# Seven-product blocks: products that need no sum first, K before Q in a level, four state updates to a bank

## The chip, the cores and the metric

The kernel runs on one core of a Trainium2 chip, as one launch. The metric is the device time of that launch in microseconds. Engines are called as in the profile: PE is TensorE (PEld its weight loads), DVE is VectorE, ACT is ScalarE, POOL is GpSimd, and SP is SyncE, which here issues most of the loads. GpSimd's queue issues the stores.

## What is computed

A backbone of two layers over 1024 latent tokens and 256 context tokens of width 1024. Layer one (neighbourhood attention beside a bidirectional mLSTM) is not touched by the change. Layer two is a bidirectional HGRN2 mixer with 16 heads of 128 keys and 128 values. Cut to what matters:

```python
def _c_mixer(h_lat, h_ctx, w_in, lb, h_norm, w_out, need_ctx):
    q, f_fwd, f_bwd, i, z = _split_cols(h @ w_in, C_SIZES)       # five blocks of 2048 columns
    f = lb + (1.0 - lb) * jax.nn.sigmoid(f_pre)                  # per direction; k = 1 - f
    ...
    # per head, per direction, chunkwise over tokens:
    S = exp(bL) * S + k_decayed.T @ v                            # the state update
    o = (q * exp(b)) @ S + a @ v
    ...
    return (rms(o) * silu(z)) @ w_out
```

All arithmetic is float32. A product of float32 matrices is made from three matmuls of split operands: each operand is kept as a high part (hh, wh: the value rounded to the matmul's format) and a low part (hl, wl: the rest), and the sum hi*hi + hi*lo + lo*hi is accumulated in PSUM. In the profile these three are the lines L131 to L133 of the helper `dense`.

## The kernel before, in words

**What sets the order.** The program is traced by a tile framework. Every instruction has a priority, by its place in the program; blocks under `urgent` come ahead of everything else. At build time a planner runs the instructions through a simulated timeline and, on each engine, always takes the ready instruction of the highest priority. On the chip each engine then works through its list strictly in order, with semaphores between engines. Buffers are rings: `self.t(pool, shape, dtype, tag, bufs)` takes the next free one of `bufs` slots of that tag, and whoever reuses a slot waits for the last reader. `self.ps(tag, shape)` takes one PSUM bank (128 x 512 float32). There are two banks for "mm", two for "tr", and in each phase some for other tags: four for "x" in the seven-product stage, three for "s" and one for "acc" in the heads. When a pool is opened over the memory of pools that were closed, its first users wait; `reuse_waits="tile"` (new in the change) makes that wait go by tile, not by pool.

**End of layer one.** The last loop of layer one (lines 1671 to 1683) forms, for each of ten token tiles in the order 8, 9, 4, 5, 6, 7, 0, 1, 2, 3, the output product, the norm and the transposed, split input of layer two: `hh` and `hl`, eight blocks of 128 rows by 1280 tokens. Pools "op0" and "wo1" hold its tiles; "st" and "sx" of the next stage are laid over them. `hg_f(0)` (line 970) then makes the backward gate of head 0 into the tile F; its half F[:, 0] is loaded only later, by `hg_proj` (line 986).

**The seven-product stage** (`hg_wide`, line 1043) computes q and the forward f for all heads: 16 units, two heads of one kind each, over a 2 x 2 blocking of weights by 512 rows and 128 columns and of h by 512 rows and 512 tokens. A unit uses seven products of blocks in place of eight. Three of them take a raw block of h, with the weight pieces (0,0), (1,0) and t4; the others take one of S1 to S4, which are sums of blocks of h, made once by `half_sums` (line 998), with the pieces t1, t2, t3 and (1,1). t1 to t4 are sums of weight blocks, made on POOL from the raw ones (line 1072). S1, S2 and S4 are chained on DVE, S3 on POOL; each is then split into a high part (ACT, line 73) and a low part (DVE, line 74), and so is each weight piece. Raw weights, t-sums and the scratch of the half sums share one ring "br" of 10 slots. `more` (line 1086) loads and splits weight pieces three products ahead. A product is 12 matmuls of 512 columns; an f unit also has four context parts of 12 matmuls of 256 columns (`cpart`). A bank such as pb takes product after product, with a DVE add that reads it between them.

**The heads.** After that come 16 heads, one after another: `hg_intra` with seven levels (`hg_level`, line 1275), `hg_vz` (v and z by matmuls), `hg_close` (transposes of K), `hg_ctx`, `hg_scan`. In a level, ACT copies the needed half of K to gksel (line 1286), PE forms 16 strips (line 1256) into one "s" bank, DVE multiplies the needed halves of Q and K by the totals (line 1303), and then folds the totals (line 1307). The matmuls of `hg_vz` and `hg_f` of the next head lie between the strips as the planner fits them in.

**The scan** (`hg_scan`, line 1316) goes over eight chunks of 128 tokens. Backward, for c = 7 to 1: a matmul u (line 1323) into an "s" bank of its own, then a DVE operation that makes the next state from the last one and u (line 1325). Forward, for c = 0 to 7: three matmuls of the output (lines 1334 to 1336) into a quarter of the "acc" bank, the forward u (line 1339) into an "s" bank, and its update (line 1341). After each four chunks ACT sums the squares (line 1350) and DVE multiplies by z (line 1354), which frees the z tile: gz has one buffer, and the next head's z waits for it (line 1189).

In layer one, `ml_yt` (lines 696 to 705) is of use to the prediction: for j in 0, 1 it transposes into half j of one "tr" bank (line 701) and reads that half by ACT (line 702).

Of the kernel before, what the change touches and what calls it, by code (L numbers as in the profile page):

```python
# [10 lines left out]
F32 = mybir.dt.float32  # L11
# [34 lines left out]
class Prog:  # L46
# [948 lines left out]
        return dict(F=F, Fc=Fc, q=q)  # L995


    def half_sums(self, pool, tp):
        nc = self.nc
        hh, hl = self.hh, self.hl  # L1000
        S = {n: [self.t(pool, [P, 4, 512], F32R, f"st{n}{c}", 1) for c in "hl"] for n in range(1, 5)}

        def A(t, c, j):
            s = slice(512 * t, 512 * t + 512)
            return hh[:, 4 * c + j, s].bitcast(F32), hl[:, 4 * c + j, s].bitcast(F32)

        def done(n, j, x):
            self.split(S[n][0][:, j, :], S[n][1][:, j, :], x)

        def pair(eng, out, x, y, op):  # L1010
            e = self.t(tp, [P, 512], F32, "br", self.brs)
            eng.tensor_tensor(out=out, in0=x[0], in1=y[0], op=op)
            eng.tensor_tensor(out=e, in0=x[1], in1=y[1], op=op)
            eng.tensor_tensor(out=out, in0=out, in1=e, op=ALU.add)

        tt = nc.vector.tensor_tensor
        s1 = []
        for j in range(4):
            s1.append(self.t(tp, [P, 512], F32, "br", self.brs))
            pair(nc.vector, s1[j], A(1, 0, j), A(1, 1, j), ALU.add)  # L1020
            done(1, j, s1[j])
        s3 = []
        for j in range(2):
            s3.append(self.t(tp, [P, 512], F32, "br", self.brs))
            pair(nc.gpsimd, s3[j], A(0, 0, j), A(1, 0, j), ALU.subtract)
        for j in range(4):
            for x in A(0, 0, j):
                tt(out=s1[j], in0=s1[j], in1=x, op=ALU.subtract)
            done(2, j, s1[j])
        for j in range(4):  # L1030
            if j > 1:
                s3.append(self.t(tp, [P, 512], F32, "br", self.brs))
                pair(nc.gpsimd, s3[j], A(0, 0, j), A(1, 0, j), ALU.subtract)
            done(3, j, s3[j])
        for j in range(4):
            h, l = A(0, 1, j)
            tt(out=s1[j], in0=h, in1=s1[j], op=ALU.subtract)
            tt(out=s1[j], in0=s1[j], in1=l, op=ALU.add)
            done(4, j, s1[j])
        return S  # L1040


    def hg_wide(self, sp, tp):
        nc, a = self.nc, self.a
        hh, hl = self.hh, self.hl
        self.brs = 10
        S = self.half_sums(sp, tp)
        add = lambda out, x, y: nc.vector.tensor_tensor(out=out, in0=x, in1=y, op=ALU.add)

        def X(n):  # L1050
# [9 lines left out]
        def raws(kind, i):  # L1060
            c0 = (2048 if kind == "f" else 0) + 2 * i * P
            b = {}
            for r, c in ((0, 0), (0, 1), (1, 1), (1, 0)):
                b[(r, c)] = self.t(tp, [P, 512], F32, "br", self.brs)
                nc.sync.dma_start(
                    out=b[(r, c)].rearrange("p (k f) -> p k f", f=P),
                    in_=a["wc"][r * 512 : r * 512 + 512, c0 + c * P : c0 + c * P + P].rearrange("(k p) f -> p k f", p=P),
                )

            def sub(x, y, out=None):  # L1070
                o = self.t(tp, [P, 512], F32, "br", self.brs) if out is None else out
                nc.gpsimd.tensor_tensor(out=o, in0=x, in1=y, op=ALU.subtract)
                return o

            b["t1"] = sub(b[(0, 1)], b[(0, 0)])
            b["t2"] = sub(b[(1, 1)], b["t1"])
            b["t3"] = sub(b[(1, 1)], b[(0, 1)], None if kind == "f" else b[(0, 1)])
            b["t4"] = sub(b[(1, 0)], b["t2"])
# [14 lines left out]
            del queue[:n]  # L1093

        more(3)
        for u, (kind, i) in enumerate(units):
            def form(n):
                more(1)
                return forms.pop((u, n))
# [15 lines left out]
            def tail(t, c, ps, x):  # L1115
                o = self.t(tp, [P, 512], F32, "ct", 2)
                add(o, ps, x)
                finish(t, c, o)

            ctx = {}  # L1120

# [39 lines left out]
            prod(pc, w, 4, False)  # L1161
            tail(0, 1, pc, u2)
            cpart(1, w, 4, True)


# [109 lines left out]
    def hg_level(self, H, lev, pool):  # L1275
# [4 lines left out]

        pick = lambda t: _skew(t[:, 0, :].rearrange("p (b s i) -> p b s i", s=2, i=h), 2, n)
        out = self.ps("s", [P, 8, 64])
        with self.urgent():
            if lev < 6:
                ksel = self.t(pool, [P, n], F32, "gksel", 1)
                m = nc.scalar.copy(ksel.rearrange("p (b s i) -> p b s i", s=2, i=h), pick(K))  # L1286
                if lev == 5:
                    self.level = m
            for c in range(8):
                for b in range(2):  # L1290
                    o = c * P + b * 64
                    r = out[:, c, :]
                    if lev < 6:
                        r = r.rearrange("p (b s i) -> p b s i", s=2, i=h)
                        lhsT, rhs = ksel[:, o : o + 64], pick(Q)[:, o // (2 * h) : (o + 64) // (2 * h)]
                    else:
                        lhsT = K[:, b, o : o + 64]
                        rhs = Q[:, 1 - b, c * P + (1 - b) * 64 : c * P + (2 - b) * 64]
                    self.strip(r, b, lhsT, rhs)
            for t, o, step in ((Q, n + 1, -n - 1), (K, 1, n - 1)):  # L1300
                v = bass.AP(t.tensor, t.offset, [list(t.ap[0]), [n + h, 2], [2 * h, nb], [1, h]])
                tot = bass.AP(Tt.tensor, Tt.offset + o, [list(Tt.ap[0]), [step, 2], [2, nb], [0, h]])
                nc.vector.tensor_tensor(out=v, in0=v, in1=tot, op=ALU.mult)  # L1303
# [3 lines left out]
            nc.vector.tensor_tensor(out=H["T"][:, :, 0:nb], in0=Tv[:, :, :, 0], in1=Tv[:, :, :, 1], op=ALU.mult)  # L1307
# [8 lines left out]
    def hg_scan(self, st, H, S, pool):  # L1316
# [2 lines left out]
        Sf, Sb = S  # L1319
        sb = {7: Sb}  # L1320
        for c in range(7, 0, -1):
            u = self.ps("s", [P, P])
            nc.tensor.matmul(u, lhsT=H["kn"][c // 4][1][:, c % 4, :], rhs=v[:, c, :], start=True, stop=True)
            s = self.t(pool, [P, P], F32, "gS1", 10)
            nc.vector.scalar_tensor_tensor(
# [3 lines left out]
        for c in range(8):  # L1329
            cs = slice(c * P, (c + 1) * P)  # L1330
            if c % 4 == 0:
                o4 = self.ps("acc", [P, 4, P])
            o = o4[:, c % 4, :]
            nc.tensor.matmul(o, lhsT=H["A"][:, c, :], rhs=v[:, c, :], start=True, stop=False)  # L1334
            nc.tensor.matmul(o, lhsT=H["Q"][:, 0, cs], rhs=sb[c], start=False, stop=False)  # L1335
            nc.tensor.matmul(o, lhsT=H["Q"][:, 1, cs], rhs=Sf, start=False, stop=True)
            if c < 7:
                u = self.ps("s", [P, P])
                nc.tensor.matmul(u, lhsT=H["kn"][c // 4][0][:, c % 4, :], rhs=v[:, c, :], start=True, stop=True)
                s = self.t(pool, [P, P], F32, "gS0", 2)  # L1340
                nc.vector.scalar_tensor_tensor(
# [66 lines left out]
    def build(self):  # L1408
        tc, nc, a = self.tc, self.nc, self.a
        dma = nc.sync.dma_start  # L1410
        with ExitStack() as es:
# [271 lines left out]

            with l1:
                FF = self.hg_f(0, None, wf)
                with tc.tile_pool(name="st", bufs=1) as sp, tc.tile_pool(name="sx", bufs=1) as tp, self.pp.phase(x=4):
                    self.hg_wide(sp, tp)
                    col = lambda i: a["wc"][:, i * 2048 : i * 2048 + P]
                    wv = self.wblock(
                        self.wp, "w", [col(3), col(4)], KD, 256, [tp, self.brs, "br"], ring=self.slabs  # L1690
                    )
                pool = l1.enter_context(tc.tile_pool(name="hg", bufs=2))
                self.rawp = pool
                banks = l1.enter_context(ExitStack())
                banks.enter_context(self.pp.phase(s=3, acc=1))
# [343 lines left out]
```

## Time and profile before

| | us |
|---|---|
| median of three runs | 3423.19 |
| lowest and highest | 3419.49, 3425.61 |
| the profiled execution | 3423.08 |
| its span, first to last instruction | 3421.3 |
| seven-product stage, steady part | from about 1846 to 2199 |
| heads | from about 2199 |

In the profile's views a time is in us from the span's start. A timeline row is: start, length, engine, line, operation, out<-in, shapes, count, and in brackets the idle time of the engine before it with what ended it. In a waits row stand who waited, for whom, the total, how many times, and the longest. Names are those of the program's tiles: "br" the ring of raw weights, "st1h" the high part of S1, "gK", "gQ", "gS" the K, Q and state of a head, "x", "mm", "s", "acc", "tr" the PSUM tags.

### The profile page before, as it was taken

The page shows a single profiled execution, that of the slowest core. Times are in us where ns is not written, and L with a number is a line of the kernel's source. Part 1 is how long each engine was busy: PE and PEld are TensorE (multiplying, and loading weights), DVE is VectorE, ACT ScalarE, POOL GpSimd, SP SyncE. Part 2 cuts the span into 40 slices and gives each one's busy share as a digit, 9 for nine tenths or more (in the row PEclk, how much of TensorE's full clock was granted, in tenths as well). Part 3 has the DMA queues.
Part 4 walks back from the last instruction along what each step waited for, and adds up shares of the span by engine and source line. Part 5 has one row for each costly group of instructions (what it writes and reads, how often), then busy time and mean ns, then how long its engine had stood idle before and what let it go on. Part 6 is the DMA issues. An engine that isn't in the chain of part 4 may idle for free. (4 is left out here: it accounts for less than half of the span.)

```text
span 3421.3 us, 64930 instructions
## 1 busy us (share of the span) xinstructions
PE 3324.6 (97%) x24814; PEld 2927.6 (86%) x24814; DVE 2186.1 (64%) x4965; ACT 1454.6 (43%) x3389; POOL 834.7 (24%) x1215
## 2 busy tenths in 40 slices
PE   7999999999999999999997999999999999999999
PEld 6699899988899888898885888888888889889887
DVE  5346666666645576686667555665676576667757
ACT  5335554445534444454453333333333333333343
POOL 2222222222221121221015333112332242233110
PEclk9999999999999999999998999999999999999999
DMA  7612322223234443444742322322222233333357
GB/s 246 233 50 82 86 83 72 82 71 91 82 93 128 127 136 107 124 142 140 244 123 74 105 101 98 106 67 83 88 94 91 81 98 84 85 86 92 83 173 207
DMA packets 338103, 379.82 MB, mean 111 GB/s; under 512 B 34600, under 2 KB 269800, under 8 KB 336768
## 3 DMA queue, kind: packets, MB, share of 16 engines
q1 hardware_dynamic: 286032, 236.73, 23.6%
q0 software_dynamic: 51760, 138.94, 12.8%
q8 instruction: 195, 3.19, 0.4%
q14 instruction: 116, 0.95, 0.1%
HBM read 272.31 MB, written 103.08 MB: 110 GB/s over the span
## 5 line engine op out<-in xcount | busy, mean ns | idle before, releaser
L131 PE MATMUL mm<-wh,hh 128*128 128x256 f32 (+1 forms) x1504 | 464.2, 309 | 1.9 <-DVE graw L1535 0.7
L132 PE MATMUL mm<-wl,hh 128*128 128x256 f32 (+1 forms) x1504 | 462.9, 308 | 0.0
L133 PE MATMUL mm<-wh,hl 128*128 128x256 f32 (+1 forms) x1504 | 459.9, 306 | 0.0
L131 PE MATMUL mm<-hh,wh 128*128 128x512 f32 (+1 forms) x1096 | 400.3, 365 | 12.8 <-ACT wh L73 12.2
L133 PE MATMUL mm<-hh,wl 128*128 128x512 f32 (+1 forms) x1096 | 396.1, 362 | 3.1 <-DVE wl L74 3.1
L132 PE MATMUL mm<-hl,wh 128*128 128x512 f32 (+1 forms) x1096 | 396.9, 362 | 1.6 <-DVE hl L318 1.6
L131 PEld LDWEIGHTS mm<-wh,hh 128*128 128x128 f32 x1504 | 283.6, 189 | 21.1 <-ACT ev L352 3.4
L132 PEld LDWEIGHTS mm<-wl,hh 128*128 128x128 f32 x1504 | 283.6, 189 | 12.6 <-issue 0.7
L133 PEld LDWEIGHTS mm<-wh,hl 128*128 128x128 f32 x1504 | 283.5, 188 | 12.0 <-issue 0.5
L131 PE MATMUL mm<-wzh,hh 128*128 128x256 f32 x960 | 275.0, 287 | 0.7 <-DVE gz L1189 0.4
L132 PE MATMUL mm<-wzl,hh 128*128 128x256 f32 x960 | 275.2, 287 | 0.0
L133 PE MATMUL mm<-wzh,hl 128*128 128x256 f32 x960 | 274.8, 286 | 0.0
L131 PEld LDWEIGHTS mm<-hh,wh 128*128 128x128 f32 x1096 | 207.5, 189 | 47.9 <-ACT wh L73 12.6
L133 PEld LDWEIGHTS mm<-hh,wl 128*128 128x128 f32 x1096 | 207.2, 189 | 33.8 <-DVE wl L74 3.8
L132 PEld LDWEIGHTS mm<-hl,wh 128*128 128x128 f32 x1096 | 207.5, 189 | 31.9 <-DVE hl L318 4.3
L1286 ACT COPY gksel<-gK 128x1024 f32<-128x1024 f32 x96 | 110.8, 1154 | 193.8 <-PE s L1256 112.9
L131 PEld LDWEIGHTS mm<-wzh,hh 128*128 128x128 f32 x960 | 183.4, 191 | 2.7 <-DVE gz L1189 0.9
L132 PEld LDWEIGHTS mm<-wzl,hh 128*128 128x128 f32 x960 | 183.6, 191 | 1.6
L133 PEld LDWEIGHTS mm<-wzh,hl 128*128 128x128 f32 x960 | 183.4, 191 | 0.9
L1303 DVE TENSOR_TENSOR gQ<-gQ,gF 128x1024 f32<-128x1024 f32 x112 | 142.0, 1268 | 46.5 <-PE s L1256 46.1
L74 DVE TENSOR_TENSOR wl<-wraw,wh 128x512 fp32r<-128x512 f32 x176 | 120.0, 689 | 77.9 <-ACT wh L73 75.4
L1303 DVE TENSOR_TENSOR gK<-gK,gF 128x1024 f32<-128x1024 f32 x112 | 143.0, 1276 | 5.3 <-DVE gF L1307 0.5
(557 smaller groups left out, 8607.9 us busy)
## 6 DMA issues: line engine op xcount, KB each, us to landing
wraw<-in_wab_dram SPq DMA_DIRECT2D x108, 256.0 KB
wraw<-yd SPq DMA_DIRECT2D x92, 256.0 KB
br<-in_wc_dram SPq DMA_DIRECT2D x64, 256.0 KB
md<-ev POOLq DMA_DIRECT2D x60, 256.0 KB, 2.7
wraw<-in_wc_dram SPq DMA_DIRECT2D x120, 128.0 KB
mloz<-md SPq DMA_DIRECT2D x40, 256.0 KB
s<-gyt POOLq DMA_DIRECT2D x36, 256.0 KB, 5.0
adar<-in_wada_dram SPq DMA_DIRECT2D x16, 512.0 KB
```

The lines of the kernel that those rows point to most:

```text
L74: nc.vector.tensor_tensor(out=lo, in0=x, in1=hi.bitcast(F32), op=ALU.subtract)
L131: mm(ps, lhsT=lh(k), rhs=rh(k), start=(start and k == 0), stop=False, skip_group_check=skip)
L132: mm(ps, lhsT=lh(k), rhs=rl(k), start=False, stop=False, skip_group_check=skip)
L133: m = mm(ps, lhsT=ll(k), rhs=rh(k), start=False, stop=(stop and k == nk - 1), skip_group_check=skip)
L1286: m = nc.scalar.copy(ksel.rearrange("p (b s i) -> p b s i", s=2, i=h), pick(K))
L1303: nc.vector.tensor_tensor(out=v, in0=v, in1=tot, op=ALU.mult)
```

## The change

Four groups of edits:

- **Start of a unit.** The products go (0,0), (1,0), t4, then t2, t3, t1, then (0,1) for f and (1,1); before it was (0,0), t2, (1,0), t3, t1, t4. t4 gets a bank of its own (pd, tag "mm") instead of adding to pb. The raw blocks are loaded in the order (0,0), (1,0), (0,1), (1,1); f units come before q units.
- **Half sums.** The first three weight pieces are asked for before `half_sums` is called. The half sums no longer use the ring "br" (now 11 slots): the running sums sit in the two free halves of F[:, 0] and in u2 and u3, those of S3 in "co". The S tiles are laid out in the order 4, 3, 1, 2. Pools "st", "sx" and "hg" get `reuse_waits="tile"`. The number of operations is as before.
- **A level.** For levels 0 to 5 the multiplication of K is traced straight after the copy to gksel; Q's stays behind the strips. At level 6 the order is Q, then K.
- **The scan.** The u of chunks 7 to 4 share one "s" bank and those of 3 to 1 another; forward, 0 to 3 one and 4 to 6 another. The matmuls and the DVE updates themselves are as before.

The diff, cut to its core:

```diff
     def half_sums(self, pool, tp, F):
-        S = {n: [self.t(pool, [P, 4, 512], F32R, f"st{n}{c}", 1) for c in "hl"] for n in range(1, 5)}
+        S = {n: [self.t(pool, [P, 4, 512], F32R, f"st{n}{c}", 1) for c in "hl"] for n in (4, 3, 1, 2)}
+        x = [F[:, 0, 0:512], F[:, 0, 512:1024]] + [self.t(tp, [P, 512], F32, n, 1) for n in ("u2", "u3")]
+        def chain(eng, out, x0, x1, *rest):
+            eng.tensor_tensor(out=out, in0=x0, in1=x1[0], op=x1[1])
+            for y, op in rest:
+                eng.tensor_tensor(out=out, in0=out, in1=y, op=op)
+        for j in range(4):
+            (h, l), (h2, l2) = A(1, 0, j), A(1, 1, j)
+            chain(nc.vector, x[j], h, (l, add), (h2, add), (l2, add))
+            done(1, j, x[j])
+        for j in range(4):
+            h, l = A(0, 0, j)
+            chain(nc.vector, x[j], x[j], (h, sub), (l, sub))
+            done(2, j, x[j])
+        for j in range(4):
+            (h, l), (h2, l2) = A(0, 0, j), A(1, 0, j)
+            y = self.t(tp, [P, 512], F32, "co", 2)
+            chain(nc.gpsimd, y, h, (l, add), (h2, sub), (l2, sub))
+            done(3, j, y)
         for j in range(4):
             h, l = A(0, 1, j)
+            chain(nc.vector, x[j], h, (x[j], sub), (l, add))
+            done(4, j, x[j])
...
     def hg_wide(self, sp, tp, F):
-        self.brs = 10
-        S = self.half_sums(sp, tp)
+        self.brs = 11
...
-        units = [(kind, i) for i in range(8) for kind in "qf"]
-        order = lambda kind: [(0, 0), "t2", (1, 0), "t3", "t1", "t4"] + ([(0, 1)] if kind == "f" else []) + [(1, 1)]
+        units = [(kind, i) for i in range(8) for kind in "fq"]
+        order = lambda kind: [(0, 0), (1, 0), "t4", "t2", "t3", "t1"] + ([(0, 1)] if kind == "f" else []) + [(1, 1)]
...
         more(3)
+        S = self.half_sums(sp, tp, F)
...
-            p1, u2, u3 = [self.t(tp, [P, 512], F32, n, 1) for n in ("p1", "u2", "u3")]
-            pa, pb, pc = self.ps("mm", [P, 512]), self.ps("x", [P, 512]), self.ps("x", [P, 512])
+            p1, u2, u3 = [self.t(tp, [P, 512], F32, n, 2 if n == "p1" else 1) for n in ("p1", "u2", "u3")]
+            pa, pd = [self.ps("mm", [P, 512]) for _ in range(2)]
+            pb, pc = [self.ps("x", [P, 512]) for _ in range(2)]
             w = form((0, 0))
             prod(pa, w, (0, 0), True)
             nc.scalar.copy(p1, pa)
             cpart(0, w, 0, False)
-            prod(pb, form("t2"), 2, True)
-            add(u2, pb, p1)
             w = form((1, 0))
             prod(pa, w, (0, 1), False)
             finish(0, 0, pa)
             cpart(0, w, 4, True)
+            prod(pd, form("t4"), (1, 1), True)
+            prod(pb, form("t2"), 2, True)
+            add(u2, pb, p1)
             prod(pb, form("t3"), 3, False)
             add(u3, pb, p1)
+            tail(1, 0, pd, u3, p1)
             prod(pc, form("t1"), 1, True)
-            tail(1, 1, pc, u3)
-            prod(pb, form("t4"), (1, 1), False)
-            tail(1, 0, pb, p1)
+            tail(1, 1, pc, u3, u3)
...
     def hg_level(self, H, lev, pool):
+        def update(t, o, step):
...
+                update(K, 1, n - 1)
             for c in range(8):
                 for b in range(2):
...
-            for t, o, step in ((Q, n + 1, -n - 1), (K, 1, n - 1)):
...
+            update(Q, n + 1, -n - 1)
+            if lev == 6:
+                update(K, 1, n - 1)
...
     def hg_scan(self, st, H, S, pool):
         for c in range(7, 0, -1):
-            u = self.ps("s", [P, P])
+            if c in (7, 3):
+                u4 = self.ps("s", [P, 4, P])
+            u = u4[:, c % 4, :]
...
             if c % 4 == 0:
                 o4 = self.ps("acc", [P, 4, P])
+                u4 = self.ps("s", [P, 4, P])
...
-                u = self.ps("s", [P, P])
+                u = u4[:, c % 4, :]
...
-                with tc.tile_pool(name="st", bufs=1) as sp, tc.tile_pool(name="sx", bufs=1) as tp, self.pp.phase(x=4):
-                    self.hg_wide(sp, tp)
+                with tc.tile_pool(name="st", bufs=1, reuse_waits="tile") as sp, tc.tile_pool(name="sx", bufs=1, reuse_waits="tile") as tp, self.pp.phase(x=4):
+                    self.hg_wide(sp, tp, FF[0])
...
-                pool = l1.enter_context(tc.tile_pool(name="hg", bufs=2))
+                pool = l1.enter_context(tc.tile_pool(name="hg", bufs=2, reuse_waits="tile"))
```

More of the change, by code (lines that the diff above doesn't have):

```diff
@@ L995, in hg_proj, with half_sums @@
         return dict(F=F, Fc=Fc, q=q)
-    def half_sums(self, pool, tp):
+    def half_sums(self, pool, tp, F):
         nc = self.nc
         hh, hl = self.hh, self.hl
-        S = {n: [self.t(pool, [P, 4, 512], F32R, f"st{n}{c}", 1) for c in "hl"] for n in range(1, 5)}
+        S = {n: [self.t(pool, [P, 4, 512], F32R, f"st{n}{c}", 1) for c in "hl"] for n in (4, 3, 1, 2)}
+        x = [F[:, 0, 0:512], F[:, 0, 512:1024]] + [self.t(tp, [P, 512], F32, n, 1) for n in ("u2", "u3")]
         def A(t, c, j):
@@ L1004, in A @@
             s = slice(512 * t, 512 * t + 512)
[L1005 to L1014, printed above, removed]
@@ L1016, in half_sums @@
-        tt = nc.vector.tensor_tensor
-        s1 = []
-        for j in range(4):
[L1019 to L1025, printed above, removed]
+            return [y[:, 4 * c + j, s].bitcast(F32) for y in (hh, hl)]
@@ new lines, in chain, with done @@
+        def chain(eng, out, x0, x1, *rest):
+            eng.tensor_tensor(out=out, in0=x0, in1=x1[0], op=x1[1])
+            for y, op in rest:
+                eng.tensor_tensor(out=out, in0=out, in1=y, op=op)
+        def done(n, j, y):
+            self.split(S[n][0][:, j, :], S[n][1][:, j, :], y)
+        add, sub = ALU.add, ALU.subtract
+        for j in range(4):
+            (h, l), (h2, l2) = A(1, 0, j), A(1, 1, j)
+            chain(nc.vector, x[j], h, (l, add), (h2, add), (l2, add))
+            done(1, j, x[j])
@@ L1026, in half_sums @@
         for j in range(4):
-            for x in A(0, 0, j):
-                tt(out=s1[j], in0=s1[j], in1=x, op=ALU.subtract)
-            done(2, j, s1[j])
+            h, l = A(0, 0, j)
+            chain(nc.vector, x[j], x[j], (h, sub), (l, sub))
+            done(2, j, x[j])
         for j in range(4):
[L1031 to L1034, printed above, removed]
+            (h, l), (h2, l2) = A(0, 0, j), A(1, 0, j)
@@ L1035, in half_sums, with hg_wide @@
+            y = self.t(tp, [P, 512], F32, "co", 2)
+            chain(nc.gpsimd, y, h, (l, add), (h2, sub), (l2, sub))
+            done(3, j, y)
         for j in range(4):
             h, l = A(0, 1, j)
-            tt(out=s1[j], in0=h, in1=s1[j], op=ALU.subtract)
-            tt(out=s1[j], in0=s1[j], in1=l, op=ALU.add)
-            done(4, j, s1[j])
+            chain(nc.vector, x[j], h, (x[j], sub), (l, add))
+            done(4, j, x[j])
         return S
-    def hg_wide(self, sp, tp):
+    def hg_wide(self, sp, tp, F):
@@ L1062, in raws @@
             b = {}
-            for r, c in ((0, 0), (0, 1), (1, 1), (1, 0)):
+            for r, c in ((0, 0), (1, 0), (0, 1), (1, 1)):
                 b[(r, c)] = self.t(tp, [P, 512], F32, "br", self.brs)
@@ L1113, in finish, with tail @@
                 nc.gpsimd.dma_start(out=d[h, :, 512 * t : 512 * t + 512], in_=o)
[L1115 to L1118, printed above, removed]
+            def tail(t, c, ps, x, out):
+                add(out, ps, x)
+                finish(t, c, out)
             ctx = {}
@@ L1161, in hg_wide @@
             prod(pc, w, 4, False)
-            tail(0, 1, pc, u2)
+            tail(0, 1, pc, u2, u2)
             cpart(1, w, 4, True)
@@ L1282, in hg_level @@
         out = self.ps("s", [P, 8, 64])
+        def update(t, o, step):
+            v = bass.AP(t.tensor, t.offset, [list(t.ap[0]), [n + h, 2], [2 * h, nb], [1, h]])
+            tot = bass.AP(Tt.tensor, Tt.offset + o, [list(Tt.ap[0]), [step, 2], [2, nb], [0, h]])
+            nc.vector.tensor_tensor(out=v, in0=v, in1=tot, op=ALU.mult)
         with self.urgent():
```

5 lines of the change are left out of this document (1 added, 4 removed).

## The prediction, made before the change was run

> **What bounds the kernel now.** I read the page first, then a table of four windows around layer two, then the waits of TensorE and of the DMA queue there, then timelines of one head.
>
> ```profile
> span 3421.3 us, 64930 instructions
> ## 1 busy us (share of the span) xinstructions
> PE 3324.6 (97%) x24814; PEld 2927.6 (86%) x24814; DVE 2186.1 (64%) x4965; ACT 1454.6 (43%) x3389; POOL 834.7 (24%) x1215
> ```
>
> TensorE is the bound: 97% busy. The change adds and removes no matmul, so it can only move idle time of TensorE, and time at a reduced clock. The windows (columns: length, busy time and count of each engine, granted clock, DMA share, GB/s) show where these lie in layer two:
>
> ```profile
> 1798.00:1812.30 14.30, 10.29 (x36) 6.20 (x34) 12.02 (x20) 6.74 (x20) 10.93 (x11) 0.88 0.05 19
> 1812.30:1846.00 33.70, 12.96 (x30) 8.69 (x29) 29.98 (x38) 12.73 (x24) 21.09 (x11) 0.60 0.22 63
> 1846.00:2199.00 353.00, 353.00 (x1730) 297.07 (x1729) 199.77 (x280) 124.18 (x214) 127.54 (x139) 1.00 0.30 100
> 2199.00:3217.00 1018.00, 981.77 (x9931) 903.28 (x9929) 685.86 (x1087) 365.12 (x775) 278.80 (x384) 1.00 0.30 87
> ```
>
> Row three is the steady part of the seven-product blocks, without idle time. About 384 of its 1730 matmuls are the half-wide context ones; counted half, a 512-wide matmul takes 353/1538 = 0.23 us. Row two is the blocks' start: 30 matmuls, 6.9 us of work, in 33.7 us, so 26.8 us are lost. Row four is the heads: 36 us idle.
>
> **Part one: the blocks' start.** What TensorE waits for there (who, whom, us in total, times, longest), and the DMA queue's longest wait for a POOL instruction:
>
> ```profile
> PE mm L131 <- ACT wh L73: 12.2, 1, 12.2
> PE x L131 <- ACT wh L73: 5.4, 2, 3.9
> PE mm L133 <- DVE wl L74: 3.1, 1, 3.1
> ```
>
> ```profile
> SPq L1065 <- POOL br L1014: 18.6, 1, 18.6
> ```
>
> The first weight's DMA waits until a POOL sum (L1014) gives up a "br" slot, since the half sums use that ring and come first in program order. The weight, its split and the first matmul follow late: 12.2 us. Then the clock is 0.60 and the weight pieces come one by one.
>
> The change issues the first block's four DMAs before the sums, gives the sums other scratch (u2, u3 and the free half of F), and starts the block with (0,0), (1,0) and t4, which read h alone. When may those DMAs start? The same pool's first write today:
>
> ```profile
> 1787.50 0.69 DVE L1012 TENSOR_TENSOR br<-hh 128x512 f32<-128x512 f32 x1 [3.51 <-PE mm L925]
> ```
>
> It waited for the last matmul on the old weights below the pool; so 1 MB of weights can start by about 1787, 25 us before they are wanted. Nothing stands behind them on SP, whose next DMA is the same one. On POOL four subtractions now go ahead of the twelve operations of S3:
>
> ```profile
> L1072 POOL TENSOR_TENSOR br<-br,br x64: 1262/1314/7067, 1828.0 to 2156.1; 128x512 f32<-128x512 f32 x64
> ...
> L1028 DVE TENSOR_TENSOR br<-br,hh x4: 676/1210/1744, 1815.2 to 1823.0; 128x512 f32<-128x512 f32 x4
> ```
>
> They are 4 x 1.31 = 5.3 us on POOL, hidden if the weights land by 1792. If not, the norm's small POOL operations for the last tokens stand behind them: 0 to 5 us, which I take as 0 and keep for the range.
>
> What is late next is VectorE. It is busy for 29.98 of the 33.7 us in row two, and the change leaves those 38 operations in place: S2, S3 and S4 and all low halves, with sums that double (0.68 to 1.74) beside POOL work. So S4, read by a block's last product, is not ready much before 1812.3 + 30 = 1842. TensorE now has work until then: three products without sums (36 x 0.23 = 8.3 us), context parts beside two of them (24 half-wide, 2.8 us), then t2, t3 and t1 (8.3 us) as S2, S3 and S1 arrive, and the f-block's remaining context parts (2.8 us): 22 us, and some of the next block's first products, 27 us in all where 6.9 were done. **Gain 20 us.** Upper bound 31 (all 26.8, and the 14.30 - 10.29 = 4.0 us idle in row one, which t4 could fill); lower bound 8, the first three products alone.
>
> In the steady part t3 now follows t2 directly, and both use the bank pb with an add (u2) between. t1 has its own bank and its weights are split ahead, so it covers the add; if that cover fails, 16 blocks wait about 1 us each. I take 0 and keep 0 to 5 for the range. Pieces, splits and adds are as many as before. The waits by tile in pool "hg" let head 0 begin earlier, under blocks where TensorE is full: 0.
>
> **Part two: K ahead of Q.** VectorE's order around two levels of head 7, and behind it ScalarE's last read of a z bank:
>
> ```profile
> 2680.83 0.69 DVE L1354 TENSOR_TENSOR gA<-acc,gz 128x512 f32<-128x512 f32 x1 [0.27 <-ACT gjk L1350]
> 2681.56 0.42 DVE L1189 TENSOR_TENSOR gz<-gsg,mm 128x256 f32<-128x256 f32 x1
> 2681.90 1.22 DVE L1303 TENSOR_TENSOR gQ<-gQ,gF 128x1024 f32<-128x1024 f32 x1
> 2683.03 0.74 DVE L1309 COPY_PREDICATED gD<-glm,s 128x512 f32<-128x512 uint8 x1
> 2683.66 1.22 DVE L1307 TENSOR_TENSOR gF<-gF 128x1024 f32<-128x1024 f32 x1
> 2684.98 1.25 DVE L1303 TENSOR_TENSOR gK<-gK,gF 128x1024 f32<-128x1024 f32 x1
> 2686.83 1.67 DVE L1303 TENSOR_TENSOR gQ<-gQ,gF 128x1024 f32<-128x1024 f32 x1 [0.60 <-PE s L1256]
> ```
>
> ```profile
> 2666.72 0.39 ACT L1188 ACTIVATE gsg<-mm 128x256 f32<-128x256 f32 x1
> ```
>
> L1307 closes level 0; the next gK is level 1's and stands ahead of level 1's gQ, which waits for the strips. The planner already runs K first. **This edit gives 0**; K cannot go further ahead, since it needs L1307's totals.
>
> **Part three: four updates in one bank.** One head's backward scan, VectorE and TensorE (a matmul here is two passes, so x12 are six u):
>
> ```profile
> 2259.84 0.29 DVE L1217 COPY gS<-s 128x128 f32<-128x128 f32 x1 [0.15 <-PE s L1215]
> 2260.23 1.25 DVE L1325 SCALAR_TENSOR_TENSOR gS<-gS,gT,s 128x128 f32<-128x128 f32 x3
> 2261.40 0.69 DVE L1233 TENSOR_TENSOR gkn<-gK 128x512 f32<-128x512 f32 x1
> 2262.00 1.25 DVE L1325 SCALAR_TENSOR_TENSOR gS<-gS,gT,s 128x128 f32<-128x128 f32 x3
> 2263.17 0.69 DVE L1233 TENSOR_TENSOR gkn<-gK 128x512 f32<-128x512 f32 x1
> 2263.77 0.34 DVE L1325 SCALAR_TENSOR_TENSOR gS<-gS,gT,s 128x128 f32<-128x128 f32 x1
> ```
>
> ```profile
> 2259.30 0.50 PE L1215 MATMUL s<-gv,gknc 128*128 128x128 f32 x3
> 2259.64 2.39 PE L1323 MATMUL s<-gv,gkn 128*128 128x128 f32 x12
> 2262.40 0.49 PE L1323 MATMUL s<-gv,gkn 128*128 128x128 f32 x2 [0.37 <-DVE gS L1325]
> ```
>
> Today the u run up to three banks ahead, and the chain steps on VectorE alone, (1.25 - 0.35)/2 = 0.45 us each. With four u in one bank, does the next u wait until VectorE has read the last one? Layer one has that pattern: two transposes into one bank, each read by ScalarE:
>
> ```profile
> 1163.33 0.27 PE L701 MATMUL tr<-ident,mhs 128*128 128x128 f32 x1
> 1163.63 0.37 ACT L702 ACTIVATE myt<-tr,hnb 128x128 f32<-128x128 f32 x1 [0.67 <-PE tr L701]
> ...
> 1168.67 0.27 PE L701 MATMUL tr<-ident,mhs 128*128 128x128 f32 x1
> 1168.98 0.37 ACT L702 ACTIVATE myt<-tr,hnb 128x128 f32<-128x128 f32 x1 [1.81 <-PE tr L701]
> ```
>
> The second transpose, ready with the first, comes 5 us later, after the read. So I take it that u and read alternate. A step is then: wake TensorE 0.05 (2262.35 to 2262.40), the u 0.49, wake VectorE 0.04 (2259.80 to 2259.84), the update 0.35: 0.93 us. Six steps cost 2.9 us more. The two L1233 inside today's chain fit mostly into the new gaps of 0.58 us: back 0.8. The forward chain waits between steps for its output matmuls anyway; I add 0.2 for the u that now stand between those. 2.3 us a head.
>
> Does other work fill TensorE meanwhile? Mostly not: the next head's z product holds its bank from 2666.72 (read by gsg) until gz at 2681.56, which waits for gA at 2680.83, the end of this scan. So the longer chain is longer idle time. Fifteen heads have a next head behind them: **cost 15 x 2.3 = 35 us.** Today's bank waits are small:
>
> ```profile
> PE s L1323 <- DVE gS L1325: 5.5, 15, 0.4
> PE s L1256 <- DVE gS L1341: 3.5, 13, 0.6
> ```
>
> Bounds: -9 (both go and fill hides all else) to 15 x 3.5 = 53 (the 2.9 not reduced, 0.6 more ahead of the outputs). I take 35, since the alternation is nearest to L701's rows.
>
> [...]
>
> **The sum.** The profiled execution took 3423.08 us (span 3421.3 and 1.8 around it; the median of three runs is 3423.19). 3423 - 20 + 35 = 3438 us, slower by 0.4%. About 0.2%, 7 us, is what a measurement of this kernel can tell from no change.
>
> **Rivals.**
> - Start wins, scan hidden: the planner knows the alternation and keeps next-head matmuls for the scan's gaps. For: nothing in the levels needs those matmuls early. Against: the bank held for 15 us above. 3423 - 20 = 3403, with the bank waits 3394. It decides from a scan cost under 13 us, 0.9 a head.
> - They cancel: half the scan cost (17) or a full start (31): 3420.
> - The start yields little: VectorE's 29.98 us of backlog still sets when the sums come, and POOL's subtractions delay the last norm. 3423 - 8 + 35 = 3450.
>
> **How the numbers follow.** Forecast 0.42; little gain 0.13; cancel 0.17; start wins 0.28. The first two give slower 0.55, the third same 0.17, the last faster 0.28. The range reaches from 3400 (start wins, with little of the bank waits) to 3456 (the little gain, and the 5 us of the t2-t3 wait), with 2 in 10 outside. The forecast's own range is 3430 to 3452.
>
> **What would show it.** Right: the first weight DMA near 1787 and no 12 us wait at the start, 30 matmuls of row two well over 100; K and Q in the same order; L1323 and L1325 alternating about 0.93 us apart, and idle time before L1323 near 2 us a head. Wrong: several L1323 without an L1325 between them, or matmuls of the next head's z in the gaps; or the start still at clock 0.6 with VectorE full.

## The result, and the profile after

| | before | after |
|---|---|---|
| median | 3422.36 us (3419.49 to 3425.61) | 3527.84 us (3523.37 to 3531.39) |
| ratio, 95% interval | | 1.0307, 1.0289 to 1.0325 |
| span of the profiled execution | 3421.3 us | 3526.0 us |

The change makes the kernel slower by 105 us. I forecast 15 us, so the sign was right and the size was not. The page after:

```profile
span 3526.0 us, 64773 instructions
PE 3387.7 (96%) x24814; PEld 2979.1 (84%) x24814; DVE 2165.0 (61%) x4965; ACT 1454.1 (41%) x3389; POOL 816.3 (23%) x1215
```

The matmuls are as many as before (24814), yet TensorE is busy 3387.7 - 3324.6 = 63 us longer for the same work; by an estimate further down at most 54 of these are a lower clock. Over the whole profiled execution the granted clock is 0.980, before it was 0.995. The four windows around layer two (columns as before) show where:

```profile
1798.00:1824.00 26.00, 23.29 (x107) 18.74 (x106) 22.57 (x38) 12.93 (x30) 16.77 (x13) 0.92 0.06 20
1824.00:1846.00 22.00, 13.96 (x58) 10.76 (x57) 22.00 (x25) 7.69 (x14) 12.68 (x9) 0.77 0.19 58
1846.00:2185.00 339.00, 337.98 (x1650) 284.51 (x1648) 179.12 (x273) 118.91 (x205) 117.81 (x134) 1.00 0.30 100
2190.00:3321.00 1131.00, 1044.79 (x9987) 950.80 (x9985) 681.96 (x1096) 369.59 (x790) 268.37 (x390) 0.95 0.27 78
```

The start is better: 107 + 58 = 165 matmuls between 1798 and 1846, where there were 36 + 30 = 66, and TensorE is idle there for 10.8 us instead of 24.8. The heads are worse: 86 us idle instead of 36, and a granted clock of 0.95 instead of 1.00. What TensorE waits for, after (who, whom, us in total, times, longest):

```profile
PE s L1325 <- DVE gS L1327: 22.3, 46, 3.3
PE s L1342 <- DVE gS L1344: 18.1, 11, 2.3
PE s L1209 <- ACT gknc L1204: 16.4, 11, 2.3
PE s L1250 <- DVE gQ L1281: 15.6, 10, 2.3
PE acc L1338 <- DVE gS L1327: 7.0, 16, 0.4
PE s L1342 <- DVE gS L1327: 6.6, 15, 0.4
PE x L132 <- DVE st2l L74: 6.5, 2, 5.3
```

L1325 and L1342 are the u of the backward and forward scan, L1327 and L1344 their updates. One backward scan, TensorE's timeline and then VectorE's:

```profile
2699.94 0.49 PE L1325 MATMUL s<-gv,gkn 128*128 128x128 f32 x2
2700.87 0.49 PE L1325 MATMUL s<-gv,gkn 128*128 128x128 f32 x2 [0.44 <-DVE gS L1327]
2701.80 0.49 PE L1342 MATMUL s<-gv,gkn 128*128 128x128 f32 x2 [0.44 <-DVE gS L1327]
2702.66 0.49 PE L1325 MATMUL s<-gv,gkn 128*128 128x128 f32 x2 [0.37 <-DVE gS L1327]
2703.59 0.79 PE L1325 MATMUL s<-gv,gkn 128*128 128x128 f32 x2 [0.44 <-DVE gS L1327]
2704.82 0.80 PE L1338 MATMUL acc<-gS,gQ 128*128 128x128 f32 x2 [0.44 <-DVE gS L1327]
2705.41 0.64 PE L1339 MATMUL acc<-gS,gQ 128*128 128x128 f32 x2
...
2708.11 1.98 PE L1250 MATMUL s<-gq,gkn 128*64 128x64 f32 x32
...
2715.96 0.39 PE L1339 MATMUL acc<-gS,gQ 128*128 128x128 f32 x2
```

```profile
2699.54 0.35 DVE L1327 SCALAR_TENSOR_TENSOR gS<-gS,gT,s 128x128 f32<-128x128 f32 x1
2700.47 0.35 DVE L1327 SCALAR_TENSOR_TENSOR gS<-gS,gT,s 128x128 f32<-128x128 f32 x1 [0.58 <-PE s L1325]
2701.40 0.35 DVE L1327 SCALAR_TENSOR_TENSOR gS<-gS,gT,s 128x128 f32<-128x128 f32 x1 [0.58 <-PE s L1325]
```

The alternation is there as forecast, one step in 0.93 us (2699.54, 2700.47, 2701.40). What I had not forecast is the clock over the same stretch (behind the last bracket):

```profile
2700.00:2703.50 3.50, 1.90 (x8) 1.13 (x8) 1.87 (x5) 0.00 (x0) 1.47 (x2) 0.97 0.23 71
2703.50:2710.50 7.00, 6.47 (x52) 5.84 (x53) 3.47 (x6) 0.00 (x0) 4.55 (x9) 0.53 0.35 116
2710.50:2715.00 4.50, 1.91 (x13) 1.34 (x11) 3.50 (x8) 1.84 (x9) 1.79 (x4) 1.00 0.19 58
```

From the last u on, with the fifth gap behind it, the clock is 0.53 for 7 us, and the outputs and the next head's first strips run in it: an output's two passes end after 0.64 us (2705.41), where they take 0.39 us (2715.96) at a granted clock of 1.00.

### The profile page after: what moved, and what is told of

Its sections match the earlier page's. It is cut to its first block, busy times and chain, and to the rows that moved or that the text cites. A ratio compares the mean times of both kernels' runs of the same rounds, so it can differ in the third digit from the quotient of the medians.

```text
span 3526.0 us, 64773 instructions
## 1 busy us (share of the span) xinstructions
PE 3387.7 (96%) x24814; PEld 2979.1 (84%) x24814; DVE 2165.0 (61%) x4965; ACT 1454.1 (41%) x3389; POOL 816.3 (23%) x1215
## 5 line engine op out<-in xcount | busy, mean ns | idle before, releaser
L131 PE MATMUL mm<-hh,wh 128*128 128x512 f32 (+1 forms) x1160 | 423.8, 366 | 5.2 <-DVE og L959 3.2
L133 PE MATMUL mm<-hh,wl 128*128 128x512 f32 (+1 forms) x1160 | 421.7, 364 | 0.8 <-DVE wl L74 0.8
L132 PE MATMUL mm<-hl,wh 128*128 128x512 f32 (+1 forms) x1160 | 422.2, 364 | 0.0
L131 PEld LDWEIGHTS mm<-hh,wh 128*128 128x128 f32 x1160 | 219.4, 189 | 43.0 <-ACT ev L371 4.2
L133 PEld LDWEIGHTS mm<-hh,wl 128*128 128x128 f32 x1160 | 219.6, 189 | 34.4 <-DVE wl L74 1.6
L132 PEld LDWEIGHTS mm<-hl,wh 128*128 128x128 f32 x1160 | 219.7, 189 | 31.1 <-DVE hl L318 0.2
L1281 DVE TENSOR_TENSOR gQ<-gQ,gF 128x1024 f32<-128x1024 f32 x112 | 139.3, 1244 | 53.8 <-PE s L1250 53.4
L1281 DVE TENSOR_TENSOR gK<-gK,gF 128x1024 f32<-128x1024 f32 x112 | 144.2, 1288 | 4.4
```

What stands on the lines that cost most here:

```text
L131: mm(ps, lhsT=lh(k), rhs=rh(k), start=(start and k == 0), stop=False, skip_group_check=skip)
L132: mm(ps, lhsT=lh(k), rhs=rl(k), start=False, stop=False, skip_group_check=skip)
L133: m = mm(ps, lhsT=ll(k), rhs=rh(k), start=False, stop=(stop and k == nk - 1), skip_group_check=skip)
```

## The experiments

The runs of "before" beside which each kernel stands have medians of 3423 to 3426 us.

**The scan edit undone.** A bank of its own for each u again; the rest of the change stays.

```diff
-            if c in (7, 3):
-                u4 = self.ps("s", [P, 4, P])
-            u = u4[:, c % 4, :]
+            u = self.ps("s", [P, P])
```

> The changed kernel with a bank for each u of the scan again (the rest of the change stays). Theory (the shared bank makes u and update alternate; that and what follows from it is the whole loss of about 7.4 us a head, 15 x 7.4 = 111 us, while the blocks' start gained about 10): 3422 - 10 = 3412 us, between 3405 and 3420. Rival (the loss comes from the K/Q edit or from the reuse of pool hg by tile): 3500 or more.

3416.94 us, ratio 0.9975 (0.9963 to 0.9988). All of the loss, 3527.8 - 3416.9 = 111 us, comes from the scan edit. This kernel is the base for what follows; its page and TensorE's waits:

```profile
span 3409.0 us, 64911 instructions
PE 3324.6 (98%) x24814; PEld 2930.4 (86%) x24814; DVE 2171.9 (64%) x4965; ACT 1454.3 (43%) x3389; POOL 832.2 (24%) x1215
```

```profile
PE acc L1334 <- DVE gA L1354: 9.1, 15, 0.7
PE s L1250 <- DVE gQ L1229: 9.1, 12, 0.9
PE acc L1335 <- DVE gS L1325: 6.8, 15, 0.7
PE s L1323 <- DVE gS L1325: 5.6, 15, 0.4
PE s L1250 <- DVE gS L1341: 3.2, 12, 0.5
PE s L1250 <- DVE gQ L1281: 2.3, 1, 2.3
PE s L1209 <- ACT gknc L1204: 2.0, 2, 1.4
```

**The scan edit alone, and the K/Q edit alone, on the kernel before.**

```diff
-            u = self.ps("s", [P, P])
+            if c in (7, 3):
+                u4 = self.ps("s", [P, 4, P])
+            u = u4[:, c % 4, :]
```

> The kernel before with the scan edit alone. Theory (all of the loss is the shared bank): 3422 + 111 = 3533 us, 3520 to 3545. Rival (the loss needs the other edits: K ahead of Q, pool hg by tile): under 3460, by my prediction's 2.3 us a head 3457.

3551.17 us, ratio 1.0372 (1.0357 to 1.0388): the loss needs none of the other edits. It is 126 us, 15 more than beside them and 6 above the theory's range; why was not tried.

```diff
+                update(K, 1, n - 1)
             for c in range(8):
...
-            for t, o, step in ((Q, n + 1, -n - 1), (K, 1, n - 1)):
+            update(Q, n + 1, -n - 1)
```

> The kernel before with the K/Q edit alone. Theory (the order was K first already): 3422 us, within 7. Rival (update of K inside the urgent block delays the strips): 3430 or more; a gain below 3415 would say that K did go ahead.

3424.75 us, ratio 1.0002 (0.9992 to 1.0011): nothing. VectorE's list of instructions is the same, in the same order.

**The bank shared without alternation.** The four u of a bank stand ahead of the four updates.

```diff
             if c in (7, 3):
                 u4 = self.ps("s", [P, 4, P])
+                for e in range(c, c - 4 if c == 7 else 0, -1):
+                    nc.tensor.matmul(u4[:, e % 4, :], ...)
...
+                for e in range(c, min(c + 4, 7)):   # forward: the same
```

> The changed kernel; the four u of a bank are issued together, ahead of the four updates that read them, so the bank is shared but nothing need alternate. Theory (the alternation is the cost, not the bank itself): 3400 to 3420 us, as with a bank for each. Rival (holding one bank for four updates, or the order that the planner finds with it, is the cost): 3500 or more.

3476.93 us, ratio 1.0158 (1.0141 to 1.0175). This fell between the theories: 60 us of the 111 stay. The page, a line of the timeline and the largest waits (here L1338 is the forward u, L1328 the backward update, L1340 the first output matmul):

```profile
PE 3325.9 (96%) x24814; PEld 2942.1 (85%) x24814; DVE 2156.4 (62%) x4965; ACT 1455.1 (42%) x3389; POOL 818.4 (24%) x1215
```

```profile
2759.54 1.73 PE L1325 MATMUL s<-gv,gkn 128*128 128x128 f32 x14
```

```profile
PE s L1338 <- DVE gS L1328: 30.9, 15, 2.3
PE acc L1340 <- DVE gA L1359: 22.1, 9, 2.5
```

Seven u run together (14 passes in 1.73 us, where the kernel before needs 2.39 us for twelve), and TensorE's busy time is back at 3325.9 us. The clock is not all the way back: 0.989 over the profiled execution, between 0.980 (after) and 0.995 (scan edit undone). So the loss of clock does not go with the alternation alone; that the busy time is back all the same I put down to the u that run closer together (0.49 us for a lone u after, 1.73/7 = 0.25 us here), which no run shows by itself. The rest of the loss is idle time, 3473.6 - 3325.9 = 148 us against 84. I read the waits as follows, which the trace alone does not show: a head takes four banks for its u and there are three, so the forward u wait for the end of the backward chain; and the next head's first strips get a bank before the outputs, so they no longer fill the wait between the two halves of the outputs. Three kernels try this.

**Fewer state banks, a second output bank, late strips**, each on the kernel with the u ahead.

```diff
-                banks.enter_context(self.pp.phase(s=3, acc=1))
+                banks.enter_context(self.pp.phase(s=2, acc=1))   # first kernel
+                banks.enter_context(self.pp.phase(s=2, acc=2))   # second
...
-        with self.urgent():   # third: the 16 first strips, line 1235
+        if True:
```

> The kernel with the u of a bank ahead (3477 us), with two banks for states, strips and levels instead of three, and one bank left unused. Theory (with four updates in one bank the third bank comes free early, and the next head's first strips are put ahead of the outputs instead of into the wait between the two halves of the outputs): the strips must again wait for the first forward bank, lie in that wait, and 2.2 us a head come back: 3440 us, 3430 to 3455. Rival (fewer banks only add waits): 3480 or more.

> The kernel with the u of a bank ahead (3477 us), with two banks for states, strips and levels, and the bank that this frees given to the outputs (two instead of one). Theory (with nothing between the two halves of the outputs, the second waits up to 2.5 us for the multiply that reads the first; 22.1 us over the heads): that wait goes, and 3440 to 3455 us are left, or below 3430 if the strips also move back. Rival (the loss is the chain of states, not the outputs' bank): 3470 or more.

> The kernel with the u of a bank ahead (3477 us), with the next head's first 16 strips without their priority, so that they come only when nothing older is ready. Theory (it is their place ahead of the outputs that costs): they fall into the wait between the halves of the outputs: 3440 us, 3430 to 3455. Rival (their place does not matter, or a late strip delays the levels behind it): 3477 or more.

3459.21, 3456.98 and 3453.10 us; ratios 1.0096 (1.0081 to 1.0111), 1.0090 (1.0070 to 1.0110) and 1.0079 (1.0062 to 1.0096). The first two end 4 and 2 us above the theory's ranges, the third inside: 18, 20 and 24 us come back. The strips' place counts here, but not in the way that the theory has it: with late strips the wait between the halves (L1340) falls only from 22.1 to 17.6 us, while those for gknc, gEc and gQ (L1281) fall from 37.0 to 14.5. None of the three kernels comes near 3417.

**Unused matmuls in the gaps**, on the changed kernel. In the first kernel they read the new state, in the second the old one.

```diff
             nc.tensor.matmul(u, ...)
+            pf = self.ps("tr", [P, 2, P])
+            for j in range(2):
+                nc.tensor.matmul(pf[:, j, :], lhsT=H["kn"][c // 4][1][:, c % 4, :], rhs=sb[c], ...)
```

> The changed kernel with two matmuls more behind each update of the backward chain (identity by the new state, into a bank that VectorE does not read), which compute nothing that is used: they put work of TensorE into the gaps of the alternation. Theory (the gaps of 0.44 us, one after another, halve TensorE's clock, and the work behind them is slow: 3387.7 - 3324.6 = 63 us of the loss): TensorE's busy time without the fillers' goes back to about 3325 us, and the time falls to 3460 to 3490 us although work is added. Rival (the loss is idle time of the longer chain, the clock does not matter): 3528 us or more, by up to 15 x 14 x 0.22 = 46 us.

3532.96 us, ratio 1.0309 (1.0292 to 1.0326), with a clock of 0.995 in place of 0.98. The unused pair stood ahead of the next u here and made a step 1.38 us long, so the time cannot tell the theories apart. The trace tells something else. Two steps of one head, and the window over its backward scan:

```profile
2704.00 0.71 PE L1333 MATMUL tr<-gS,ident 128*128 128x128 f32 x4 [0.44 <-DVE gS L1327]
2704.55 0.39 PE L1325 MATMUL s<-gv,gkn 128*128 128x128 f32 x2
2705.37 0.71 PE L1333 MATMUL tr<-gS,ident 128*128 128x128 f32 x4 [0.44 <-DVE gS L1327]
```

```profile
2701.20:2709.70 8.50, 6.39 (x43) 5.23 (x43) 3.65 (x9) 0.00 (x0) 6.16 (x11) 1.00 0.24 82
```

Four gaps of this scan last 0.44 us, as in the changed kernel. But such a step has 0.94 us of matmuls (2704.00 to 2704.94) in its 1.38 us, where the changed kernel has 0.49 in 0.93, and the clock stays at 1.00. So it is not the length of a gap by itself that brings the clock down; in these two kernels the clock goes with the share of time that TensorE works (at 0.49/0.93 = 53% of it the clock falls to 0.53, at 0.94/1.38 = 68% it stays at 1.00).

> The changed kernel with the same two unused matmuls a step, now standing behind each u and reading the old state, so that they run while VectorE updates and the step keeps its length (0.93 us, at most 1.0). Theory (the reduced clock behind the alternation is 63 us of the loss): 3465 to 3490 us, granted clock over 0.99. Rival (the clock costs little, the longer chain is all): 3528 us, within 10.

3490.60 us, ratio 1.0192 (1.0173 to 1.0211): 37 us faster than the changed kernel, with 448 matmul passes more, 0.6 us above the theory's range. The clock is 0.995 in the profiled execution and 0.991 to 0.992 in the three others, where the changed kernel has 0.980 to 0.981. The page, and the steps, again 0.93 us (2677.40, 2678.32, 2679.25):

```profile
span 3483.3 us, 65711 instructions
PE 3384.1 (97%) x25262; PEld 2987.6 (86%) x25262; DVE 2163.6 (62%) x4965; ACT 1454.5 (42%) x3389; POOL 812.7 (23%) x1215
```

```profile
2677.40 0.34 DVE L1330 SCALAR_TENSOR_TENSOR gS<-gS,gT,s 128x128 f32<-128x128 f32 x1
2678.32 0.35 DVE L1330 SCALAR_TENSOR_TENSOR gS<-gS,gT,s 128x128 f32<-128x128 f32 x1 [0.58 <-PE s L1325]
2679.25 0.73 DVE L1330 SCALAR_TENSOR_TENSOR gS<-gS,gT,s 128x128 f32<-128x128 f32 x2 [0.58 <-PE s L1325]
```

At 1.73/14 = 0.12 us a pass the unused ones are some 54 us of the busy time (an estimate), which leaves 3330: nearly all of the 63 us is gone, and the idle time, 99 us, is down from 138, as the unused matmuls stand in it. The banks are shared and the steps as long as in the changed kernel, so between these two kernels the clock goes with TensorE's idle time in the scan (0.980 with the gaps empty, 0.995 with the unused matmuls in them), not with the shared bank as such.

**One scan at a time**, on the changed kernel.

```diff
-            u = u4[:, c % 4, :]                # forward (first kernel) or backward (second)
+            u = self.ps("s", [P, P])
```

> The changed kernel with shared banks in the backward scan alone; each forward u has its own bank again. Theory (the backward chain has nothing between its steps, so its alternation brings the gaps and the low clock): three quarters of the 111 us, 3480 to 3510 us. Rival (the forward chain, between the outputs, costs as much): 3470 or less.

> The changed kernel with shared banks in the forward scan alone; each backward u has its own bank again. Theory (the outputs between the forward steps hide most of their alternation; what remains is the earlier strips): 3430 to 3455 us. Rival (the forward chain costs as much as the backward one): 3470 or more.

3466.47 us, ratio 1.0125 (1.0108 to 1.0142), and 3455.88 us, ratio 1.0097 (1.0077 to 1.0118). Beside 3416.9 the backward scan costs 50 us and the forward one 39. The first time is below its theory's range and within the rival's bound, the second 1 us above its theory's range: the forward scan is not the small part that the theories made of it. 22 us more appear only with both. Their pages, backward first:

```profile
span 3467.7 us, 64790 instructions
PE 3369.0 (97%) x24814; PEld 2968.8 (86%) x24814; DVE 2175.0 (63%) x4965; ACT 1455.0 (42%) x3389; POOL 815.1 (24%) x1215
```

```profile
span 3450.8 us, 64884 instructions
PE 3348.8 (97%) x24814; PEld 2942.7 (85%) x24814; DVE 2159.2 (63%) x4965; ACT 1451.7 (42%) x3389; POOL 830.8 (24%) x1215
```

Backward alone: 44 us of longer busy time and 14 of idle time (98.7 - 84.4), at a clock of 0.982. Forward alone: 24 and 18, but at 0.994, hardly below the 0.995 of the kernel with the scan edit undone. So most of these 24 us are not the clock ((0.995 - 0.994) x 3450.8 = 3.5 us, an estimate); a lone u behind a wait took 0.49 us and one in a row of seven 1.73/7 = 0.25 us, but that this makes up the 24 us was not shown.

**Late strips with the alternation in place**, on the changed kernel, and together with the unused matmuls (the edits as above).

> The changed kernel with the next head's first 16 strips without their priority. Theory (put ahead of the outputs, at half clock, they cost about what they cost in the kernel with the u ahead, 24 us): 3500 to 3510 us. Rival (with the alternation in place, the gaps take them as well in one place as in another): 3520 to 3535.

> The changed kernel with the unused matmuls behind each backward u and without the priority of the first strips. Theory (clock 37 us, strips 24, and what remains is the longer chain): 3528 - 37 - 24 = 3467 us, 3455 to 3475, so that the chain alone costs 50 us beside 3417. Rival (clock and strips are one cost, as the strips only cost because they run slow): 3480 to 3491.

3530.58 us, ratio 1.0315 (1.0301 to 1.0329), and 3495.37 us, ratio 1.0212 (1.0198 to 1.0226). The first lies in the rival's range, the second above both forecasts. The theory falls: in the changed kernel the place of the strips costs nothing.

**The start: S3's sums left out, then moved to VectorE; and pool "hg" without the reuse by tile**, all on the kernel with the scan edit undone.

```diff
-            chain(nc.gpsimd, y, h, (l, add), (h2, sub), (l2, sub))
-            done(3, j, y)
+            done(3, j, x[j])                                          # left out
+            chain(nc.vector, y, h, (l, add), (h2, sub), (l2, sub))    # moved
```

> The changed kernel without the scan edit (3417 us), without the 16 sums on POOL that make S3; S3 is split from the same tiles as S2, so its values are not those of the reference. Theory (VectorE's operations take 1.75 us instead of 0.68 beside those sums, and this is why the start gained 9 us and not 20): 3403 to 3410 us, and the low halves of S2 come some 8 us earlier. Rival (VectorE's number of operations sets the start whatever POOL does): 3415 to 3420.

3404.65 us, ratio 0.9942 (0.9926 to 0.9959): 12 us faster than with the sums. (The edit takes out 12 operations on POOL, not 16.) TensorE's wait for S2's low halves, 6.5 us, is gone, and the clock between 1812.3 and 1846 is 1.00; with the sums on POOL it is 0.85.

> The changed kernel without the scan edit (3417 us), the sums of S3 on VectorE instead of POOL; all of the computation is there. Theory (POOL's sums double VectorE's operations, which costs more than the 12 x 0.60 = 7.2 us that they take on VectorE itself): 3406 to 3413 us. Rival (VectorE is full there, so its 12 operations more take the gain back): 3415 to 3422.

3407.16 us, ratio 0.9962 (0.9948 to 0.9975). This is the lowest median of a kernel that computes everything; against the one with POOL's sums (0.9975) the intervals overlap, so a gain over it is not shown by the times. The traces go the same way: the wait for S2's low halves is 1.3 us instead of 6.5. Below are, in this order, VectorE after, POOL after, and VectorE with the sums moved, where POOL has nothing to do between 1822.7 and 1834.2:

```profile
1825.59 1.77 DVE L1011 TENSOR_TENSOR u<-u,hl 128x512 f32<-128x512 f32 x1
1827.29 1.75 DVE L74 TENSOR_TENSOR wl<-br,wh 128x512 fp32r<-128x512 f32 x1
```

```profile
1819.02 4.68 POOL L1065 TENSOR_TENSOR br<-br,br 128x512 f32<-128x512 f32 x1 [5.44 <-DVE wl L74]
1825.20 1.61 POOL L1011 TENSOR_TENSOR co<-co,hh 128x512 f32<-128x512 f32 x1
1826.78 1.71 POOL L1009 TENSOR_TENSOR co<-hh,hl 128x512 f32<-128x512 f32 x1
```

```profile
1825.57 0.68 DVE L1011 TENSOR_TENSOR u<-u,hl 128x512 f32<-128x512 f32 x1
```

> The changed kernel without the scan edit (3417 us) and without the reuse by tile of pool hg. Theory (that edit gives nothing): 3417 us, within 5. Rival (it is part of the start's gain, since head 0 begins earlier by it): 3421 to 3428.

3413.73 us, ratio 0.9974 (0.9964 to 0.9983), beside 0.9975: in pool hg the reuse by tile gives nothing.

## Why the prediction came out as it did

**The failed step is the scan's cost, "15 x 2.3 = 35 us".** It was 111 us. The alternation and its step of 0.93 us were right. Three things were wrong in the term.

First, it priced gaps as idle time alone. In the profiled executions the scan edit costs 3526.0 - 3409.0 = 117 us: 63 of longer busy time, and (3526.0 - 3387.7) - (3409.0 - 3324.6) = 54 idle. By the mean clock, (1 - 0.980) x 3526.0 = 71 us were not granted, and (1 - 0.995) x 3409.0 = 17 without the scan edit. So at most 54 of the 63 are the clock (an estimate; some of it falls into idle time), and no run shows what the rest is. The clock had no place in this term, though the prediction names it at its start, and the run with the gaps filled shows that it belongs there: after the change gaps of 0.37 to 0.44 us are followed by 7 us at 0.53, and with the unused matmuls in the gaps the mean clock is 0.995 in place of 0.980.

Second, "The forward chain waits between steps for its output matmuls anyway; I add 0.2" a head. Forward alone cost 39 us, 2.6 a head.

Third, the sum stopped at the chain. Of the idle time, the waits for states (gS) rise from 6.8 + 5.6 + 3.2 = 15.6 us to 22.3 + 18.1 + 7.0 + 6.6 = 54.0, by 38; that part is near my 35, but by luck, since 24.7 of the 54.0 are waits of the forward u (L1342), which I had at 0.2 a head. But two waits elsewhere in the head, for gknc and for gQ at L1281, rise from 4.3 to 32.0 us. That the planner, with other banks free, had used up the z matmuls that covered them is argued from their place and not shown. In return the waits for gA and for gQ at L1229, 18 us together, are nearly gone from the list.

**The start: 8 us, not 20** (3424.69 - 3416.94, with the scan edit undone; the interval of the ratio allows 4 to 13). The first weight DMA went out at 1779.75, earlier than my 1787, so it did not wait for the last matmul on the old weights (L925, begun at 1786.47). The 12 us wait is gone, and from 1812.3 to 1846 there are 114 matmuls instead of 30, as forecast. VectorE was what came late next, as the text says; but S2's low halves came at up to 1.76 us each instead of 0.68, TensorE waited 6.5 us for them, and the clock in the second window was 0.77. I had named the doubling beside POOL's sums and then left the work in place as if it cost no more than before. That the lower bound was 8 is luck: it was to hold for the first three products alone, and more than these ran early. The wait that I feared between t2 and t3 is not there: between 1846 and 2190 TensorE has only three waits, 1.7 us together.

**K ahead of Q, and the reuse by tile in pool hg: 0**, as forecast, each by a run of its own. What the reuse by tile in pools st and sx gives was not tried alone.

**The rivals.** All of them varied the start or the hiding of the scan; none let the scan cost more than its own gaps. The upper bound of 53 us came from the backward steps alone, and so the range ended 72 us too low. One sum among them is wrong as well: a full start gives 3423 - 31 + 35 = 3427, not 3420.

**Open:** why the scan edit costs 15 us more without the other edits; what moved the two waits for gknc and gQ; what the 24 us of longer busy time are with the forward scan alone; and why the kernel with the u ahead still loses 36 us when its strips are late. By its clock of 0.992, about (0.995 - 0.992) x 3453 = 10 us of these can be the clock (an estimate).

## What to carry to other kernels

Before several steps of a chain share a PSUM bank, ask whether writer and reader will alternate; if they do, price the gaps twice, once as idle time and once as slow matmuls behind them, and look at the granted clock of the stretch: here the idle time was 54 us, the longer busy time 63 us, and the clock 0.53 for 7 us behind the steps of the scan shown. Ask too whether a tile that holds a bank longer moves who gets the next bank: here two waits outside the chain rose from 4.3 to 32.0 us, so that a sum over the chain alone fell short, though that the banks moved them was not shown. And work put on POOL was not free here, where VectorE was busy for all of the 22.00 us from 1824 to 1846: VectorE's operations took 1.75 us beside POOL's sums and 0.68 us without them, and the 12 sums cost no more on VectorE (3407.16 us against 3416.94).

## What the runs showed of the hardware

Idle time of 0.37 to 0.44 us between pairs of matmul passes of 0.49 us, four times in a row, was followed by 7 us at a granted clock of 0.53 (after, 2703.5 to 2710.5), with a fifth gap of 0.44 us within them. With 0.94 us of matmuls between idle times of 0.44 us, the clock stayed at 1.00. Two unused matmuls in each gap brought the mean clock of the profiled execution from 0.980 to 0.995 and the time down by 37 us. A 128x512 VectorE operation took 1.75 us beside a row of POOL operations of 1.6 to 1.7 us each, and 0.68 us with POOL idle. In the trace after it is also once the other way round: VectorE's operations from 1819.46 to 1822.47 took 0.69 us each, while one POOL operation on as many elements, begun at 1819.02, took 4.68 us; POOL's times are rough in the profile.
